# Second attention layer of a two-layer encoder: the heads as a written-out pipeline of 64 query-tile units

## The chip, the cores and the metric

One core of one Trainium2 chip runs the whole kernel. The metric is the device time of one execution in microseconds (us): 682.92 us is the median of three runs before the change (682.80 to 683.17). Five engines work side by side, each through its own list of instructions: TensorE (PE in the profile; PEld is its weight load), VectorE (DVE), ScalarE (ACT), GpSimd (POOL) and the queue that issues transfers (SP).

## The reference

Two encoder layers over 512 tokens of width 1024, in float32. The change lies in the second one, multi-head latent attention with 16 heads:

```python
def mixer_mla(xn, w_in, q_norm, w_qb, kv_norm, w_kvb, w_out):
    c_q, c_kv, k_rope, z = jnp.split(xn @ w_in, [384, 640, 672], axis=-1)
    q = (rmsnorm(c_q, q_norm) @ w_qb).reshape(B, S, H, 64 + 32)
    q_nope, q_pe = jnp.split(q, [64], axis=-1)
    q_pe = apply_rope(q_pe, cos, sin)
    kv = (rmsnorm(c_kv, kv_norm) @ w_kvb).reshape(B, S, H, 64 + 64)
    k_nope, v = jnp.split(kv, [64], axis=-1)
    k_pe = apply_rope(k_rope[:, :, None, :], cos, sin)
    ...
    o = block_attention(q, k, v)          # softmax(q k^T * 96 ** -0.5) v
    return (o.reshape(B, S, H * 64) * jax.nn.silu(z)) @ w_out
```

Around it stand the first layer (neighbourhood attention), the output projections, and after each layer a gated embedding: `h + sigmoid(rmsnorm(h) @ w_gate) * (p @ w_proj)`.

## The kernel before

**Precision.** Every float32 operand is split into two parts, `hi` and `lo` (`split`, L83 to L87: ScalarE copies to `hi`, VectorE or GpSimd subtracts to `lo`), and each product is three matmuls: hi by hi, hi by lo, lo by hi. A weight tile comes through `load_w` (L75 to L77): a transfer to `wraw`, the `hi` cast on ScalarE (L76, `whi`), the subtraction on GpSimd (L77, `wlo`). The pool `wp` has three buffers each of `wraw`, `whi` and `wlo`, so a fourth weight's cast can begin only when the matmuls that read one of the three are done.

**PSUM.** Eight banks of 128x512: two under the name `ps_mm` (projections), two `ps_S` (scores), three `ps_T` (transposes), one `ps_O` (a head's output).

**The second layer's heads (`mla_heads`, `mla_head`).** Heads go in eight pairs, and pairs in four groups of two.

- `group(g)` loads the group's weights (`mla_qr` for the rotary query part, `mla_kv` for keys and values, `mla_qn` for the queries), makes the rotary part (nine matmuls of 512 columns into one `ps_mm` bank; a copy, a lane shuffle, two products and a sum on ScalarE, VectorE and GpSimd; split to `rh`, `rl`), and the values of four heads (four times six matmuls of 256 columns, each evacuated by itself to a tile `vt`).
- `project(j)` makes one pair's operands: nine query matmuls into a `ps_mm` bank, evacuated by four instructions to `qe` and `qo` (the pair's even and odd head, hi and lo), six key matmuls into another, to `ke` and `ko`, and small transfers of rows of `rh` and `rl` into `qe` and `qo`.
- `attend(j)` runs the pair's two heads. A head has four query tiles. A tile's work: three score matmuls into `ps_S`; row maximum on VectorE (L594); exponential with row sum on ScalarE (L596); reciprocal (L597); scaling on GpSimd (L598); four transposes into `ps_T` (L122); split to `pt_hi` and `pt_lo`. After the four tiles come eight output matmuls into `ps_O`, four by `pt_hi` and four by `pt_lo`. `combine` (L182 to L185) evacuates the output, `gated` (L190 to L194) multiplies it by the gate `z` and splits it to `o1h`, `o1l`.

The gates of eight pairs (`z_phase`, 24 matmuls each) are made before the heads, the eighth between the first projection and the pairs. Behind the heads `ple` multiplies the layer's embedding (48 matmuls), then `out_proj` projects the output.

**What sets the order.** The program text calls for group, attention and projection one after the other; a scheduler with a timeline of its own then decides where each instruction stands on its engine, and may mix the scores of one head with the transposes of another. At run time each engine goes through its list in that order; an instruction waits on semaphores for its operands and for the buffer that it writes.

## Time and profile before

| | |
|---|---|
| median of 3 runs (range) | 682.92 us (682.80 to 683.17) |
| the profiled execution's own time | 682.41 us |
| span of the profile (first to last instruction) | 680.6 us |
| granted TensorE clock, mean over the span | 0.998 |
| stretch of the heads: first rotary matmul to the end of their mixing with `out_proj` | 404.8 to 590.0 us |

The profile's page gives the busy time of each engine, a chain of waits followed back from the last instruction, and groups of instructions by line. Answers on a stretch of time or a tile come from the same trace. A row of a timeline begins with start and length in us, then engine, line, operation, tile written <- tiles read, partitions x elements and the count merged. Matmuls overlap: the time that one costs in a row of them is the distance of two starts, not its length.

### The profile page before, as it was taken

The numbers are of one execution on the slowest core, as the hardware profiler recorded it, in microseconds if no ns is written. First come the engines' busy times: TensorE is split into PE (matmuls) and PEld (weight loads), VectorE is DVE, ScalarE is ACT, GpSimd is POOL, SyncE is SP. The second block draws the span as 40 slices with busy tenths as digits, with TensorE's granted clock in tenths as the row PEclk, the third lists the DMA queues.
The fourth block names the chain that finished last, engine by engine and source line by source line (L and its number), as shares of the span: only waits on it lengthen the run. The fifth ranks groups of instructions, "written<-read, shape, count | busy, mean of one in ns | idle before, by whom it ended". The sixth has DMA issues, their size and how long they took to land.

```text
span 680.6 us, 10112 instructions
## 1 busy us (share of the span) xinstructions
PE 660.7 (97%) x3552; PEld 564.2 (83%) x3552; DVE 369.4 (54%) x833; ACT 406.7 (60%) x808; POOL 395.2 (58%) x308
## 2 busy tenths in 40 slices
PE   6999999999999999999999999999999999999995
PEld 5888898988988888788999886787888777887885
DVE  6361555648646615724615404778888885046333
ACT  6753766657667643633444543888798877426423
POOL 0394556565766575832045634867799766658511
PEclk9999999999999999999999999999999999999999
DMA  8944214223142146434242252202121202584122
GB/s 276 375 139 145 89 41 136 87 93 111 40 137 74 63 176 231 166 110 149 93 128 93 75 160 80 82 23 93 26 70 39 86 1 78 203 296 154 60 78 93
DMA packets 30370, 79.10 MB, mean 116 GB/s; under 512 B 3952, under 2 KB 7280, under 8 KB 30320
## 3 DMA queue, kind: packets, MB, share of 16 engines
q1 hardware_dynamic: 30320, 78.47, 34.6%
q8 instruction: 28, 0.46, 0.3%
q14 instruction: 22, 0.18, 0.1%
HBM read 66.92 MB, written 8.39 MB: 111 GB/s over the span
## 4 chain that ended last, share of the span: by engine, by line
PE 87%; ACT 5%; DVE 3%; issue 2%; DMA 1%; POOL 1%; SPq 0%; POOLq 0%; DVEq 0%; ACTq 0%
PE ps_mm L96 60%; PE ps_S L96 10%; PE ps_T L122 5%; PE ps_O L96 4%; PE ps_O L357 2%; PE ps_mm L167 2%; PE ps_T L345 1%; ACT ex L596 1%; ACT whi L76 1%; PE ps_S L310 1%; PE ps_S L309 1%; DVE mx L594 1%; PE ps_T L96 1%; DMA wraw<-pT 1%; DMA wraw<-mla_c 0%
## 5 line engine op out<-in xcount | busy, mean ns | idle before, releaser
L77 POOL TENSOR_TENSOR wlo<-wraw,whi 128x1024 fp32r<-128x1024 f32 (+3 forms) x93 | 211.0, 2283 | 102.6 <-ACT whi L76 69.4
L76 ACT ACTIVATE whi<-wraw 128x1024 fp32r<-128x1024 f32 (+3 forms) x93 | 92.0, 999 | 80.1 <-PE ps_mm L96 20.1
L598 POOL TENSOR_TENSOR ex<-ex,rc 128x512 f32<-128x512 f32 x64 | 66.2, 1047 | 21.0 <-DVE rc L597 15.9
L96 PE MATMUL ps_mm<-whi,hnT 128*128 128x512 f32 (+1 forms) x272 | 69.7, 377 | 0.0
L96 PEld LDWEIGHTS ps_mm<-whi,hnT 128*128 128x128 f32 x272 | 49.5, 188 | 9.5
L332 POOL TENSOR_TENSOR ex<-ex,rc 128x128 f32<-128x128 f32 (+1 forms) x64 | 34.3, 560 | 37.9 <-DVE rc L328 36.4
L594 DVE TENSOR_REDUCE mx<-ps_S 128x1 f32<-128x512 f32 x64 | 43.7, 685 | 15.3 <-PE ps_S L96 14.4
L596 ACT ACTIVATE ex<-ps_S,mx 128x512 f32<-128x512 f32 x64 | 44.1, 689 | 8.2 <-DVE mx L594 6.7
L85 DVE TENSOR_TENSOR pt_lo<-ps_T,pt_hi 128x512 fp32r<-128x512 f32 x64 | 43.0, 679 | 5.0 <-ACT pt_hi L83 4.6
L327 ACT ACTIVATE ex<-ex,mx 128x128 f32<-128x128 f32 (+1 forms) x64 | 30.2, 473 | 21.5 <-DVE mx L323 21.2
L83 ACT ACTIVATE pt_hi<-ps_T 128x512 fp32r<-128x512 f32 x64 | 37.0, 598 | 7.6 <-PE ps_T L122 7.3
L96 PE MATMUL ps_mm<-xh,whi 128*128 128x512 f32 x152 | 41.0, 400 | 0.1
L96 PE MATMUL ps_mm<-wlo,hnT 128*128 128x512 f32 (+1 forms) x136 | 40.6, 379 | 0.0
L96 PE MATMUL ps_mm<-xh,wlo 128*128 128x512 f32 x152 | 39.2, 392 | 0.0
L96 PE MATMUL ps_mm<-xl,whi 128*128 128x512 f32 x152 | 38.7, 392 | 0.0
L122 PE MATMUL ps_T<-ident,ex 128*128 128x128 f32 x256 | 36.3, 273 | 0.2 <-DVE pt_lo L85 0.2
L122 PEld LDWEIGHTS ps_T<-ident,ex 128*128 128x128 f32 x256 | 30.7, 140 | 6.7 <-issue 0.7
L437 DVE TENSOR_TENSOR sg<-pe,sg 128x512 f32<-128x512 f32 (+1 forms) x17 | 12.5, 733 | 39.6 <-ACT sg L436 39.6
L96 PEld LDWEIGHTS ps_mm<-xl,whi 128*128 128x128 f32 x152 | 28.1, 188 | 5.7
L96 PEld LDWEIGHTS ps_mm<-xh,wlo 128*128 128x128 f32 x152 | 28.1, 188 | 5.5
L190 POOL TENSOR_TENSOR u<-u,z 128x512 f32<-128x512 f32 x16 | 20.6, 1290 | 19.6 <-DVE u L185 18.8
L106 POOL TENSOR_TENSOR rs<-ss,half 128x1 f32<-128x1 f32 x20 | 10.8, 549 | 35.9 <-DVE ss L105 34.7
(268 smaller groups left out, 1666.6 us busy)
## 6 DMA issues: line engine op xcount, KB each, us to landing
pe<-pe SPq DMA_DIRECT2D x32, 256.0 KB, 3.1
wraw<-na_qk SPq DMA_DIRECT2D x16, 512.0 KB, 3.3
wraw<-gate SPq DMA_DIRECT2D x16, 512.0 KB, 3.3
wraw<-na_v SPq DMA_DIRECT2D x8, 512.0 KB, 3.3
wraw<-na_o SPq DMA_DIRECT2D x8, 512.0 KB, 3.5
wraw<-mla_z SPq DMA_DIRECT2D x8, 512.0 KB, 3.6
wraw<-mla_o SPq DMA_DIRECT2D x8, 512.0 KB, 3.9
wraw<-na_z SPq DMA_DIRECT2D x6, 512.0 KB, 6.3
```

Source lines behind the costliest of these rows:

```text
L76: nc.scalar.activation(hi[:, c], raw[:, c], AF.Copy)
L77: (rest or nc.gpsimd).tensor_tensor(out=lo[:, c], in0=raw[:, c], in1=hi[:, c].bitcast(F32), op=ALU.subtract)
L83: nc.scalar.activation(hi, src, AF.Copy, scale=scale)
L85: nc.vector.tensor_tensor(out=lo, in0=src, in1=hi.bitcast(F32), op=ALU.subtract)
L96: last = nc.tensor.matmul(out, l, r, start=i == 0, stop=i == n - 1)
L122: self.nc.tensor.transpose(t[:, i * P:(i + 1) * P], b, self.ident)
L190: nc.gpsimd.tensor_tensor(out=u, in0=u, in1=z, op=ALU.mult)
L327: self.last_exp = nc.scalar.activation(e, e, AF.Exp, bias=mx[:, qt:qt + 1], accum_out=sm[:, qt:qt + 1])
L332: nc.gpsimd.tensor_tensor(out=e, in0=e, in1=rc[:, qt:qt + 1].to_broadcast([P, e.shape[1]]), op=ALU.mult)
L594: nc.vector.reduce_max(mx[:, c], sp, axis=AX.X, negate=True)
L596: nc.scalar.activation(ex, sp, AF.Exp, bias=mx[:, c], accum_out=sm[:, c])
L598: nc.gpsimd.tensor_tensor(out=ex, in0=ex, in1=rc[:, c].to_broadcast([P, S]), op=ALU.mult)
```

## The change

`mla_heads` is written anew. `group`, `project`, `attend` and `mla_head` are gone. A loop over 69 steps takes their place; its first 64 each handle one query tile (a unit) of one head. In step `i` TensorE gets, in this order: the scores of unit `i`, some matmuls of the next pair's operands (`pieces`), the transposes of unit `i-3`, and at two of four steps half of an earlier head's output (the half by `pt_hi` or the half by `pt_lo`). Each of these blocks is put behind the last matmul before it (`issue_after`), which fixes the order on TensorE alone; the other engines' order remains the scheduler's.

Further: the weights of a group are loaded in two halves (`parts=2`); two token tiles of values share a bank and are evacuated together; the rotary product with the cosine reads the bank instead of the copy; the products of `ple` are cut into 16 half blocks and put into the last steps, with the two output halves of a token tile stored together; for the first pair the values take `ps_S` banks, and the eighth gate stands wholly before the first scores.

```diff
+        def part(key, bank, terms, a0, a1):
+            if a0 == 0:
+                PS[key] = self.psum(bank)
+            for i in range(a0, a1):
+                self.last_mm = nc.tensor.matmul(PS[key], *terms[i], start=i == 0, stop=i == len(terms) - 1)
+            return PS.pop(key) if a1 == len(terms) else None
...
+        def load(key, ap, n):
+            W_[key] = self.load_w(ap, n, parts=2)
...
+        def rope(g, a0, a1):
+            psr = part(("r", g), "mm", q_terms(W_["qr", g], 0), a0, a1)
+            if psr is None:
+                return
...
             nc.scalar.activation(xr, psr, AF.Copy)
             nc.vector.stream_shuffle(sw, xr, swap)
-            nc.vector.tensor_tensor(out=xr, in0=xr, in1=rc_t, op=ALU.mult)
+            nc.vector.tensor_tensor(out=xr, in0=psr, in1=rc_t, op=ALU.mult)
...
+        def queries(j, a0, a1, bank="mm"):
+            g, jj = j // 2, j % 2
+            psq = part(("q", j), bank, q_terms(W_["qn", g], jj * 384), a0, a1)
+            if psq is None:
+                return
             st = sets[j % 2]
+            for dst, r in ((st["qe"], slice(0, 64)), (st["qo"], slice(64, 128))):
                 self.split(dst[0][r], dst[1][r], psq[r], QSC)
...
+        def pieces(j):
+            n, g = j + 1, j // 2 + 1
+            w = [[] for i in range(8)]
+            add = lambda i, f, *x: w[i].append(lambda: f(*x))
+            if j < 6 and j % 2 == 0:
+                add(0, queries, n, 0, 2)
+                add(1, queries, n, 2, 8)
+                add(2, queries, n, 8, 9)
+                add(2, load_kv, g)
+                add(2, keys, n, 0, 5)
+                add(3, keys, n, 5, 6)
+                add(3, load_qn, g)
+                add(3, rope, g, 0, 1)
+                add(4, rope, g, 1, 3)
+                add(5, rope, g, 3, 9)
+                add(6, values, g, 0)
+                add(6, values, g, 1)
+            elif j < 7:
+                add(0, queries, n, 0, 1)
+                add(1, queries, n, 1, 6)
+                add(2, queries, n, 6, 9)
+                if j == 6:
+                    add(2, load, "w0", a["proj"][1, 0], 1024)
+                add(2, keys, n, 0, 2)
+                add(3, keys, n, 2, 3)
+                add(4, keys, n, 3, 4)
+                add(5, keys, n, 4, 6)
+                if j == 6:
+                    add(5, load, "w1", a["proj"][1, 1], 1024)
+                    add(6, ple)
+                    add(6, ple)
...
+        for i in range(69):
+            work = []
+            if i < 64:
+                work.append(lambda: score(i))
+                work += pieces(i // 8)[i % 8]
+            elif i < 66:
+                work += [ple, ple]
+            if 3 <= i < 67:
+                work.append(lambda: turn(i - 3))
+            if i >= 7 and i % 4 in (3, 0):
+                work.append(lambda: output((i - 7) // 4, (i + 1) % 4))
+            for f in work:
+                with self.tc.issue_after(self.last_mm.ins):
+                    f()
```

`score`, `turn` and `output` hold what `mla_head` held, for one unit, one unit and half a head. Rows that precede the second layer's heads are the same on every engine.

Two places in the lists matter below. The first is TensorE in the third pair (units 16 to 23), where the next group's rotary product begins; `ps_mm_4836` are the keys of the fourth pair (its queries, `ps_mm_4770`, end just ahead), `ps_mm_4872` is the rotary product, and `ps_S` are scores. Before, the corresponding place (rotary product `ps_mm_4992`) reads:

```order
L96 MATMUL ps_O_4669<-pt_lo_4604,vt_4247 128x512
L96 MATMUL ps_O_4669<-pt_lo_4604,vt_4257 128x512
L96 MATMUL ps_S_4814<-ke00_3497,qe00_3493 128x512
L96 MATMUL ps_S_4814<-ke01_3498,qe00_3493 128x512
L96 MATMUL ps_S_4814<-ke00_3497,qe01_3494 128x512
L96 MATMUL ps_mm_4992<-cT0_3491,whi_4987 128x512 x3
L96 MATMUL ps_mm_4992<-cT1_3492,whi_4987 128x512 x3
L96 MATMUL ps_mm_4992<-cT0_3491,wlo_4988 128x512 x3
L96 MATMUL ps_S_4830<-ke00_3497,qe00_3493 128x512
```

and now:

```order
L510 MATMUL ps_mm_4770<-cT0_3491,wlo_4415 128x512
L510 MATMUL ps_mm_4836<-cT0_3491,whi_4385 128x512 x2
L510 MATMUL ps_mm_4836<-cT1_3492,whi_4385 128x512 x2
L510 MATMUL ps_mm_4836<-cT0_3491,wlo_4386 128x512
L122 MATMUL ps_T_4842<-ident_70,ex_4740 128x128 x4
L96 MATMUL ps_S_4849<-ke00_3497,qe00_3493 128x512
L96 MATMUL ps_S_4849<-ke01_3498,qe00_3493 128x512
L96 MATMUL ps_S_4849<-ke00_3497,qe01_3494 128x512
L510 MATMUL ps_mm_4836<-cT0_3491,wlo_4386 128x512
L510 MATMUL ps_mm_4872<-cT0_3491,whi_4720 128x512
L122 MATMUL ps_T_4876<-ident_70,ex_4766 128x128 x4
```

Nine rotary matmuls in one piece have become one, two and six in three steps, and the first of them follows the last query matmul after only six key matmuls, four transposes and three score matmuls.

The second place is ScalarE over the same steps. `whi_4828` and `whi_4864` are casts of the next group's key and value weights and query weights, `ex` the exponentials, `pt_hi` the split of transposes, `qe10`, `qo10`, `ke10`, `ko10` the evacuation of the fourth pair's queries and keys. Before (casts `whi_5014`, `whi_5060`):

```order
L596 ACTIVATE ex_4704,sm_4679<-ps_S_4699,mx_4678 128x512
L76 ACTIVATE whi_5014<-wraw_5013 128x1024
L83 ACTIVATE qe10_3501<-ps_mm_4957 64x512
L76 ACTIVATE whi_5060<-wraw_5059 128x768
L83 ACTIVATE ke10_3505<-ps_mm_4975 64x512
L596 ACTIVATE ex_4720,sm_4679<-ps_S_4715,mx_4678 128x512
L83 ACTIVATE pt_hi_4603<-ps_T_4662 128x4x128
L83 ACTIVATE pt_hi_4681<-ps_T_4692 128x4x128
L83 ACTIVATE qo10_3503<-ps_mm_4957 64x512
```

and now:

```order
L599 ACTIVATE ex_4766,sm_4759<-ps_S_4761,mx_4758 128x512
L83 ACTIVATE pt_hi_4744<-ps_T_4773 128x4x128
L187 ACTIVATE u_4784<-ps_O_4753 64x512
L76 ACTIVATE whi_4828<-wraw_4827 128x512 x2
L599 ACTIVATE ex_4792,sm_4759<-ps_S_4787,mx_4758 128x512
L83 ACTIVATE pt_hi_4744<-ps_T_4802 128x4x128
L83 ACTIVATE qe10_3501<-ps_mm_4770 64x512
L599 ACTIVATE ex_4814,sm_4759<-ps_S_4809,mx_4758 128x512
L76 ACTIVATE whi_4864<-wraw_4863 128x384 x2
L83 ACTIVATE pt_hi_4744<-ps_T_4842 128x4x128
L83 ACTIVATE qo10_3503<-ps_mm_4770 64x512
L83 ACTIVATE ke10_3505<-ps_mm_4836 64x512
```

Both lists have the two casts ahead of evacuations; now each cast is in two halves, and the first stands ahead of the exponential of unit 17 (`ex_4792`), whose scores TensorE finishes before the last query matmuls.

## The prediction

> **What bounds the kernel now.** I read the page first, then the windows of the heads' stretch, then TensorE's timeline, then the chain of waits where that timeline has holes.

> ```profile
> PE 660.7 (97%) x3552; PEld 564.2 (83%) x3552; DVE 369.4 (54%) x833; ACT 406.7 (60%) x808; POOL 395.2 (58%) x308
> PE 87%; ACT 5%; DVE 3%; issue 2%; DMA 1%; POOL 1%; SPq 0%; POOLq 0%; DVEq 0%; ACTq 0%
> ```

> The span is 680.6 us. TensorE has 97% of it and 87% of the chain: only its own work or its waits can move the end. The lists before and after hold the same 3552 matmuls, so its work stays; what can change is how long it waits. Busy time hides that, since matmuls overlap, so I count. The stretch (its length, then busy time and instructions of PE, PEld, DVE, ACT, POOL, then the granted clock), and its matmuls that are not 512 columns wide:

> ```profile
> 404.80:590.00 185.20, 179.16 (x940) 147.03 (x939) 131.82 (x268) 140.77 (x300) 134.39 (x108) 1.00 0.22 67
> ```

> ```profile
> L122 PE MATMUL ps_T<-ident,ex 128*128 128x128 f32 x256 | 36.3, 273 | 0.2 <-DVE pt_lo L85 0.2
> ...
> L96 PE MATMUL ps_mm<-whi,cT 128*128 128x256 f32 x64 | 10.8, 291 | 1.2 <-DVE vt L85 0.8 <-ACT xr L518 0.3
> ...
> L96 PE MATMUL ps_mm<-wlo,cT 128*128 128x256 f32 x32 | 6.4, 282 | 0.0
> ```

> That leaves 940 - 256 - 96 = 588 matmuls of 512 columns. What one costs in a row of them is the distance of starts, from TensorE's timeline where it does not wait:

> ```profile
> 505.37 0.86 PE L96 MATMUL ps_S<-ke,qe 96*128 96x512 f32 x3
> 506.07 0.60 PE L122 MATMUL ps_T<-ident,ex 128*128 128x128 f32 x4
> 506.43 0.94 PE L96 MATMUL ps_S<-ke,qe 96*128 96x512 f32 x3
> ...
> 514.07 0.64 PE L96 MATMUL ps_mm<-whi,cT 128*128 128x256 f32 x4
> 514.55 0.40 PE L96 MATMUL ps_mm<-wlo,cT 128*128 128x256 f32 x2
> 514.79 0.60 PE L122 MATMUL ps_T<-ident,ex 128*128 128x128 f32 x4
> ```

> ```profile
> 365.02 10.94 PE ps_mm L96 x48
> ```

> The second fence is a row of the chain: 48 matmuls of 512 columns in 10.94 us, 0.228 each. Three scores take 0.70 (505.37 to 506.07), four transposes 0.36, six matmuls of 256 columns 0.72, half an output 4 x 0.23 = 0.92. Work of the stretch: 588 x 0.228 = 134.1, 96 x 0.12 = 11.5, 64 x 0.36 = 23.0, together 168.6 us of 185.2. **TensorE waits about 16 us there**; that is all the change can win, and 682.9 - 16 = 667 is the floor. A hole shows how these waits come about, in the chain:

> ```profile
> 456.98 0.66 ACT ex L596 x2
> 457.64 0.95 ACT whi L76
> 458.59 0.46 ACT qe L83
> 459.05 0.74 ACT whi L76
> ...
> 460.15 0.79 ACT ex L596 x2
> ...
> 460.98 0.97 PE ps_S L96 x3
> ```

> Two weight casts (0.95 and 0.74) and an evacuation stand in ScalarE's list between two exponentials; the scores at 460.98 start right behind the second, which frees their bank. ScalarE runs its list in order, so whatever waits at its head holds all behind it. Over the stretch such casts waited for TensorE, too:

> ```profile
> L76 ACT ACTIVATE whi<-wraw 128x1024 fp32r<-128x1024 f32 (+2 forms) x17 | 15.7, 925 | 6.2 <-PE ps_mm L96 6.1
> ```

> **The change, by its steps.** A step's matmuls, first four steps of a pair that prepares a group: 0.70 + 2 x 0.23 + 0.36 + 0.92 = 2.44; 0.70 + 6 x 0.23 + 0.36 = 2.44; 0.70 + 6 x 0.23 + 0.36 = 2.44; 0.70 + 2 x 0.23 + 0.36 + 0.92 = 2.44. Each unit thus has three steps, some 7.3 us, from scores to transposes. The chain between is maximum, exponential, reciprocal and scaling:

> ```profile
> L594 DVE TENSOR_REDUCE mx<-ps_S 128x1 f32<-128x512 f32 x64 | 43.7, 685 | 15.3 <-PE ps_S L96 14.4
> L598 POOL TENSOR_TENSOR ex<-ex,rc 128x512 f32<-128x512 f32 x64 | 66.2, 1047 | 21.0 <-DVE rc L597 15.9
> L87 DVE SCALAR_TENSOR_TENSOR qo<-ps_mm,qo 64x512 fp32r<-64x512 f32 x8 | 5.6, 695 | 0.9 <-ACT qo L83 0.7
> L521 POOL TENSOR_TENSOR sw<-sw,rope_s 128x512 f32<-128x512 f32 x4 | 6.1, 1520 | 0.0
> L522 POOL TENSOR_TENSOR xr<-xr,sw 128x512 f32<-128x512 f32 x4 | 5.2, 1290 | 0.9 <-DVE xr L520 0.7
> L77 POOL TENSOR_TENSOR wlo<-wraw,whi 128x1024 fp32r<-128x1024 f32 (+3 forms) x93 | 211.0, 2283 | 102.6 <-ACT whi L76 69.4
> ```

> 0.69 + 0.9 + 0.2 + 1.05 is under 3 us, so transposes rarely wait. What binds instead are banks and ScalarE's list. Its distances of starts:

> ```profile
> 456.85 0.70 ACT L596 ACTIVATE ex<-ps_S,mx 128x512 f32<-128x512 f32 x1
> ...
> 457.51 1.08 ACT L76 ACTIVATE whi<-wraw 128x1024 fp32r<-128x1024 f32 x1
> 458.46 0.59 ACT L83 ACTIVATE qe<-ps_mm 64x512 fp32r<-64x512 f32 x1
> 458.94 0.85 ACT L76 ACTIVATE whi<-wraw 128x768 fp32r<-128x768 f32 x1
> 459.67 0.59 ACT L83 ACTIVATE ke<-ps_mm 64x512 fp32r<-64x512 f32 x1
> ```

> An exponential takes 0.66, a key-and-value cast 0.95 (1.0 in two halves, my estimate), a query cast 0.73 (0.75 in halves), an evacuation 0.48.

> *The rotary product's bank.* In pairs 2 and 4, counted from the pair's first score, the last query matmul ends at 4.88 + 0.70 + 0.23 = 5.81, and the first rotary matmul is due at 8.25. It takes the query bank, so it needs the pair's `qo` evacuated. On ScalarE the key-and-value cast has stood at the head since about 3.3: its buffer comes free with the last query matmul. From 6.0 on (0.2 for the result to land) come in order: cast 1.0, exponential 0.66, `pt_hi` 0.48, `qe` 0.48, exponential 0.66, query cast 0.75, `pt_hi` 0.48, `qo` 0.6 to its result, which makes 11.1, and VectorE's `qo` 0.70: 11.8. TensorE stands from 8.25 to 11.8: **3.5 us, twice**; all scores, transposes and outputs queue behind. If ScalarE's backlog were half, 1.2; with GpSimd late as well, 4.5. In pair 0, without transposes, the same sum gives 8.6 against 6.25: **2.4**, and 0.3 for a score bank.

> *Pair 6* (counting from 0) loads `proj` behind its queries and keys. The cast of 1.0 delays `pt_hi`, and the output half at its fourth step waits **1.3**; the second cast waits for the last key matmul ahead of an exponential, and the seventh step's scores wait **2.1**.

> *Output halves.* At the end of a pair, the first half comes 0.70 + 0.36 after the transposes that it needs, while `pt_hi` follows others on ScalarE: 0 to 0.8 each, seven times, **3**.

> *The eighth gate* now follows the first keys and takes the query bank. Its weights' buffer comes free with the rotary matmuls; from there cast 0.95, GpSimd 2.28, rotary product 1.52 and sum 1.29, which `rh`, then `ke` and `qo` follow on ScalarE (1.6), then 0.70: 10.9 after the last early gate, against 8.3 for the keys' end: **2.6** (1.5 to 3.5).

> *At nothing:* values in pairs (half the evacuations), the cosine product from the bank, loads in halves (some 14 casts more, 0.05 each) and joined stores lie beside TensorE, on engines that are busy 132 to 141 us of 185. If ScalarE were full, the halves would cost 0.7. On SP the loads' transfers need only a `wraw` buffer, which the subtraction frees several steps sooner than the casts' buffers come free, so they land ahead of the casts; behind SP's small transfers of `rh` and `rl` stand only loads for later steps.

> *The end.* `proj`'s buffers are held to the last half blocks, so `out_proj`'s first cast starts only then: 0.95 + 2.28 for the lower part, under 3.4 us of blocks and transposes and 2.7 of its first twelve matmuls. Small waits there and in pair 7: **0.8**.

> Sum: 3.5 x 2 + 2.7 + 3.4 + 3 + 2.6 + 0.8 = 19.5 us of waits in place of 16: +3.5. Against the profiled 682.41 this is 685.9; the runs' median lies 0.5 above the profiled one, so **686.5 us**. With every term at its low end the waits are some 11, at its high end 27: 678 to 694.

> [...]

> **The rivals.** *Faster: the fixed order finds its operands ready.* The place is the rotary product's first matmul and the point is `qo`: if ScalarE's list flows there and `qo` is evacuated 2.4 us after the queries' end, the 9.4 us of rotary waits go. 10 us remain, 6 under the 16 now: 677. For it: three steps between scores and transposes, engines 71 to 76% busy. Against it: the order of ScalarE's list, and 6.1 us of casts already waiting for TensorE in the old one.

> *No change:* both sets of waits come out at 16, within 1.4 us, 682.9. For it speaks that the same casts and evacuations share the same ScalarE; against it that nothing ties the two sums.

> *Slower still: the clock.* When TensorE stands, its granted clock falls, at least at the end:

> ```profile
> 670.00:681.00 11.00, 3.33 (x28) 0.86 0.26 95
> ```

> Of these 11.00 us TensorE is busy 3.33, and the clock's mean is 0.86.

> The holes of this stretch, at most 1.6 us, left it at 1.00. Holes of 3.5 are longer. If each of the two lowered it to half, matmuls at twice 0.228 for one step add some 2.4 us each: 691.

> [...]

> **How the numbers follow.** Forecast 0.46; faster 0.34; no change 0.13; clock 0.07. About 0.2%, 1.4 us, is what a measurement of this kernel tells from no change: 681.5 to 684.3. So faster 0.34, same 0.13, slower 0.53. The forecast's own range is 684.3 to 691. The faster case spreads from 667 to 681.5, mostly above 674; I leave out a little below that, and above 692. Range 674 to 692.

> **What would show it.** For the forecast: the first rotary matmul of a group idle by 2 to 4 us, released by VectorE's `qo`; ScalarE idle before the casts, released by TensorE; waits of TensorE in the stretch of 17 to 24 us. For the faster rival: no hole over 1 us behind the eighth gate, and evacuations within 2.4 us. For the clock: granted clock under 1.00 in a window between 430 and 580. The forecast is wrong if `qo` lands before the rotary matmul is due, or if TensorE's waits fall under 14 us.

## The result, and the profile after

| | before | after |
|---|---|---|
| median of 4 runs each, on one chip (range) | 682.86 us (682.56 to 683.17) | 688.52 us (687.91 to 691.05) |
| ratio to before, 95% interval | | 1.0090 (1.0064 to 1.0116) |
| the profiled execution's own time, and its span | 682.41, 680.6 us | 691.05, 689.3 us |
| mean granted clock over the span | 0.998 | 0.992 |

The kernel became 0.9% slower, 5.7 us. The profiled execution of the changed kernel is the longest of its four; the other three have a mean clock of 0.994 and take 687.91 to 688.91 us. One more stretch at half clock, which by the estimate of 1.7 us below would lower the mean clock by 0.002, fits the 0.992 and covers more than half of that difference; the other three left no trace.

The page's busy time and chain after the change:

```profile
PE 663.9 (96%) x3552; PEld 567.6 (82%) x3552; DVE 370.3 (54%) x825; ACT 408.5 (59%) x815; POOL 395.6 (57%) x323
PE 86%; ACT 7%; DVE 3%; issue 1%; DMA 1%; POOL 1%; SPq 0%; POOLq 0%; DVEq 0%; ACTq 0%
```

The shares hardly differ from before. The stretch of the heads tells more. Counted from the first rotary matmul over the same number of matmuls, 940, as the 185.20 us before (length, then busy time and instructions of each engine, then the clock):

```profile
406.67:598.60 191.93, 180.67 (x940) 149.21 (x939) 132.73 (x260) 141.04 (x302) 133.89 (x120) 0.98 0.22 72
```

It is 6.7 us longer, at a clock of 0.98. Where TensorE stands idle is told by its groups in 400 to 600 us: first the groups before the change that stand over 0.5 us (count, busy time, mean of one; then the idle time just before them and who ended it),

```profile
L96 PE MATMUL ps_S<-ke,qe 96*128 96x512 f32 x96 | 28.8, 409 | 2.1 <-ACT ex L596 1.4 <-ACT ke L83 0.7
L96 PE MATMUL ps_S<-ko,qo 128*128 128x512 f32 x96 | 28.8, 410 | 1.5 <-ACT ex L596 1.5
L96 PE MATMUL ps_O<-pt_hi,vt 128*128 128x512 f32 x64 | 18.0, 403 | 0.7 <-ACT pt_hi L83 0.7
```

(the values' 1.2 us stand in the prediction), and after it:

```profile
L510 PE MATMUL ps_mm<-cT,whi 128*128 128x512 f32 x104 | 31.3, 399 | 6.0 <-DVE qo L87 6.0
L616 PE MATMUL ps_O<-pt_hi,vt 128*128 128x512 f32 x64 | 19.2, 422 | 2.9 <-ACT pt_hi L83 2.8
L96 PE MATMUL ps_mm<-x1h,whi 128*128 128x512 f32 x16 | 4.9, 460 | 2.2 <-DVE qo L87 2.2
```

No scores wait for an exponential any more: the written-out order does what it says. In their place stand the rotary product (6.0 us in three waits, all for VectorE's `qo`), the first output halves (2.9 us, for `pt_hi`) and the eighth gate (2.2 us, for `qo` of the first queries): 11.1 us in place of 5.5.

The wait of the third pair (pair 2) in the timeline, all three engines; rows go by engine, and `[2.16 <-DVE qo L87]` is idle time ahead of an instruction and who ended it:

```profile
466.58 0.40 PE L510 MATMUL ps_mm<-cT,wlo 128*128 128x512 f32 x1
...
468.31 0.95 PE L96 MATMUL ps_S<-ke,qe 96*128 96x512 f32 x3
469.10 0.40 PE L510 MATMUL ps_mm<-cT,wlo 128*128 128x512 f32 x1
471.65 0.47 PE L510 MATMUL ps_mm<-cT,whi 128*128 128x512 f32 x1 [2.16 <-DVE qo L87]
...
465.17 1.15 ACT L76 ACTIVATE whi<-wraw 128x512 fp32r<-128x512 f32 x2 [0.84 <-PE ps_mm L510]
466.35 0.69 ACT L599 ACTIVATE ex<-ps_S,mx 128x512 f32<-128x512 f32 x1
...
467.02 0.59 ACT L83 ACTIVATE pt_hi<-ps_T 128x512 fp32r<-128x512 f32 x1
467.50 0.58 ACT L83 ACTIVATE qe<-ps_mm 64x512 fp32r<-64x512 f32 x1
467.98 0.68 ACT L599 ACTIVATE ex<-ps_S,mx 128x512 f32<-128x512 f32 x1
...
468.64 0.94 ACT L76 ACTIVATE whi<-wraw 128x384 fp32r<-128x384 f32 x2
469.47 0.59 ACT L83 ACTIVATE pt_hi<-ps_T 128x512 fp32r<-128x512 f32 x1
470.08 0.59 ACT L83 ACTIVATE qo<-ps_mm 64x512 fp32r<-64x512 f32 x1
...
468.25 0.67 DVE L87 SCALAR_TENSOR_TENSOR qe<-ps_mm,qe 64x512 fp32r<-64x512 f32 x1
...
470.81 0.69 DVE L87 SCALAR_TENSOR_TENSOR qo<-ps_mm,qo 64x512 fp32r<-64x512 f32 x1
```

The last query matmul starts at 466.58; VectorE's `qo` ends at 471.50, 4.92 us later, and the rotary product, which writes that bank, starts at 471.65. From 465.17 on ScalarE has no idle time until `qo`, and these rows start in the order of its list under the change.

The clock is the second part. Six stretches of 3.41 us, TensorE alone (length, busy time and instructions, granted clock):

```profile
414.88:418.29 3.41, 1.20 (x6) 1.00 0.27 65
418.29:421.71 3.42, 3.42 (x10) 0.50 0.30 71
469.50:472.91 3.41, 1.26 (x8) 1.00 0.44 154
472.91:476.32 3.41, 3.41 (x11) 0.50 0.37 115
510.44:513.85 3.41, 1.86 (x11) 1.00 0.07 15
513.85:517.27 3.42, 2.80 (x14) 1.00 0.36 138
```

Behind the gate's wait (2.21 us, to 417.38) and behind the wait of pair 2 (2.16 us, to 471.65) TensorE runs 3.41 us at a clock of 0.50: three scores take 1.28 us to the next start there (473.66 to 474.94), against 0.68 at a clock of 1.00 (477.41 to 478.09). Reckoned by the clock, it does in 3.41 us what 1.71 us would do. Behind the wait of pair 4 (third pair of rows) the clock stays at 1.00, though a wait of the same length stands there (2.17 us, to 514.47). So in this execution the clock takes, by this estimate, 2 x 1.7 = 3.4 us. Beside the work as the prediction prices it, 168.6 us, there remain 191.93 - 168.6 - 3.4 = 19.9 us, against 185.20 - 168.6 = 16.6 before.

The prediction calls this remainder waits, but not all of it is. By the busy times in the two rows of the stretch TensorE is idle for 191.93 - 180.67 = 11.3 us, and before the change for 185.20 - 179.16 = 6.0. The other 8.6 and 10.6 us are in large part work priced too low: the three scores at 468.31 in the timeline above, which wait for nothing, take 0.79 us to the next start and not 0.70. Averaged over all matmuls of 512 columns that follow one another without idle time, a step is 0.24 us in the traces of both kernels where 0.228 was taken, which makes 6 to 7 us.

### The profile page after: what moved, and what is told of

It reads as the page before. It is cut to its first block, busy times and chain, and to the rows that moved or that the text cites. A ratio compares the mean times of both kernels' runs of the same rounds, so it can differ in the third digit from the quotient of the medians.

```text
span 689.3 us, 10135 instructions
## 1 busy us (share of the span) xinstructions
PE 663.9 (96%) x3552; PEld 567.6 (82%) x3552; DVE 370.3 (54%) x825; ACT 408.5 (59%) x815; POOL 395.6 (57%) x323
## 4 chain that ended last, share of the span: by engine, by line
PE 86%; ACT 7%; DVE 3%; issue 1%; DMA 1%; POOL 1%; SPq 0%; POOLq 0%; DVEq 0%; ACTq 0%
PE ps_mm L96 54%; PE ps_S L96 10%; PE ps_mm L510 5%; PE ps_T L122 5%; PE ps_O L616 5%; PE ps_O L360 2%; ACT ex L599 2%; PE ps_mm L167 2%; PE ps_T L348 1%; PE ps_S L313 1%; PE ps_S L312 1%; ACT whi L76 1%; ACT pt_hi L83 1%; PE ps_T L96 1%; DMA wraw<-pT 1%
## 5 line engine op out<-in xcount | busy, mean ns | idle before, releaser
L77 POOL TENSOR_TENSOR wlo<-wraw,whi 128x1024 fp32r<-128x1024 f32 (+5 forms) x108 | 213.0, 1989 | 107.3 <-ACT whi L76 75.7
L76 ACT ACTIVATE whi<-wraw 128x1024 fp32r<-128x1024 f32 (+5 forms) x108 | 93.2, 886 | 74.8 <-PE ps_mm L96 19.8
L601 POOL TENSOR_TENSOR ex<-ex,rc 128x512 f32<-128x512 f32 x64 | 66.2, 1042 | 29.0 <-DVE rc L600 10.6
L96 PE MATMUL ps_mm<-whi,hnT 128*128 128x512 f32 (+1 forms) x272 | 69.7, 377 | 0.0
L96 PEld LDWEIGHTS ps_mm<-whi,hnT 128*128 128x128 f32 x272 | 49.5, 188 | 9.5
L335 POOL TENSOR_TENSOR ex<-ex,rc 128x128 f32<-128x128 f32 (+1 forms) x64 | 34.4, 562 | 37.9 <-DVE rc L331 36.3
L597 DVE TENSOR_REDUCE mx<-ps_S 128x1 f32<-128x512 f32 x64 | 44.0, 688 | 21.2 <-PE ps_S L96 19.7
L599 ACT ACTIVATE ex<-ps_S,mx 128x512 f32<-128x512 f32 x64 | 43.7, 683 | 13.4 <-DVE mx L597 13.2
L85 DVE TENSOR_TENSOR pt_lo<-ps_T,pt_hi 128x512 fp32r<-128x512 f32 x64 | 43.1, 685 | 11.7 <-ACT pt_hi L83 10.9
L83 ACT ACTIVATE pt_hi<-ps_T 128x512 fp32r<-128x512 f32 x64 | 37.4, 596 | 8.0 <-PE ps_T L122 7.8
L96 PE MATMUL ps_mm<-xh,whi 128*128 128x512 f32 x152 | 41.0, 400 | 0.1
L96 PE MATMUL ps_mm<-wlo,hnT 128*128 128x512 f32 (+1 forms) x136 | 40.6, 379 | 0.0
L96 PE MATMUL ps_mm<-xh,wlo 128*128 128x512 f32 x152 | 39.2, 392 | 0.0
L96 PE MATMUL ps_mm<-xl,whi 128*128 128x512 f32 x152 | 38.7, 392 | 0.0
L122 PE MATMUL ps_T<-ident,ex 128*128 128x128 f32 x256 | 38.5, 274 | 0.1
L122 PEld LDWEIGHTS ps_T<-ident,ex 128*128 128x128 f32 x256 | 31.8, 142 | 7.5 <-POOL ex L601 0.5
L510 PE MATMUL ps_mm<-cT,whi 128*128 128x512 f32 x104 | 31.3, 399 | 6.0 <-DVE qo L87 6.0
L188 DVE TENSOR_TENSOR u<-ps_O,u 64x512 f32<-64x512 f32 x32 | 22.0, 686 | 24.6 <-ACT u L187 24.1
L96 PEld LDWEIGHTS ps_mm<-xl,whi 128*128 128x128 f32 x152 | 28.1, 188 | 5.7
L96 PEld LDWEIGHTS ps_mm<-xh,wlo 128*128 128x128 f32 x152 | 28.1, 188 | 5.5
```

The costliest lines, as they stand in the source:

```text
L76: nc.scalar.activation(hi[:, c], raw[:, c], AF.Copy)
L77: (rest or nc.gpsimd).tensor_tensor(out=lo[:, c], in0=raw[:, c], in1=hi[:, c].bitcast(F32), op=ALU.subtract)
L83: nc.scalar.activation(hi, src, AF.Copy, scale=scale)
L85: nc.vector.tensor_tensor(out=lo, in0=src, in1=hi.bitcast(F32), op=ALU.subtract)
L96: last = self.last_mm = nc.tensor.matmul(out, l, r, start=i == 0, stop=i == n - 1)
L122: self.last_mm = self.nc.tensor.transpose(t[:, i * P:(i + 1) * P], b, self.ident)
```

## The experiments

Ten kernels, in three rounds on one chip each with the kernel before beside them. Its medians there are 683.24, 683.50 and 682.94 us, against 682.86 in the first comparison, which alone holds the kernel after; so a difference of times from two sets can be off by some 0.6 us. The idle columns are the groups of TensorE's rows in 400 to 600 us, as above: rotary product for `qo`, first output half for `pt_hi`, eighth gate for `qo`, scores for an exponential.

| | median (range), us | ratio to before (95%) | rotary | output | gate | scores |
|---|---|---|---|---|---|---|
| after | 688.52 (687.91 to 691.05) | 1.0090 (1.0064 to 1.0116) | 6.0 | 2.9 | 2.2 | 0.0 |
| 1 rotary product later | 683.62 (681.22 to 684.40) | 1.0002 (0.9987 to 1.0016) | 0.6 | 3.3 | 2.2 | |
| 2 casts behind | 688.63 (686.16 to 690.86) | 1.0071 (1.0047 to 1.0096) | 5.3 | 3.5 | 2.2 | |
| 3 gate's bank | 685.90 (685.05 to 688.01) | 1.0038 (1.0024 to 1.0052) | 6.0 | 2.9 | 0.0 | 0.0 |
| 4 waits filled | 686.33 (684.66 to 687.48) | 1.0041 (1.0028 to 1.0053) | 1.9 | 2.9 | 0.1 | 0.0 |
| 5 `qo` first | 685.38 (683.28 to 686.64) | 1.0024 (1.0011 to 1.0038) | 2.1 | 3.0 | 2.2 | |
| 6 = 1 + 3 | 678.83 (678.66 to 680.21) | 0.9936 (0.9922 to 0.9950) | 0.6 | 3.3 | 0.0 | 0.0 |
| 7 = 6, output half later | 675.99 (675.46 to 676.58) | 0.9890 (0.9876 to 0.9904) | 0.6 | 0.0 | 0.0 | 0.8 |
| 8 two and two | 685.12 (683.66 to 685.82) | 1.0029 (1.0020 to 1.0039) | 2.4 | 4.2 | 1.4 | |
| 9 = 8, casts behind | 686.15 (685.59 to 686.86) | 1.0047 (1.0032 to 1.0062) | 1.3 | 5.9 | 1.4 | |
| 10 = 7, two and two | 682.18 (680.96 to 682.50) | 0.9985 (0.9976 to 0.9995) | 0.0 | 3.6 | 0.0 | 2.9 |

(Empty: under 0.3 us. In run 4 the idle time is what is left beside the extra matmuls.)

### Round one: each suspect alone

**1. The rotary product one step later.**

```diff
-                add(3, rope, g, 0, 1)
-                add(4, rope, g, 1, 3)
+                add(4, rope, g, 0, 3)
```

> The rotary product starts one step later (its first matmul moves from a pair's fourth step to the fifth), nothing else moves on TensorE. Theory A (the query bank is not free yet because the evacuation of qo stands behind casts on ScalarE): the waits ahead of the first rotary matmul in pairs 0, 2 and 4 (1.9, 2.3 and 2.3 us) fall under 0.4 us each, and the half-clock window behind pair 2's wait goes with its hole: 688.5 - 6 - 1.7 = about 681, at most 683. Rival B (ScalarE is short of time in these steps, so the wait only changes its place): scores or output halves wait instead, and the time stays within 1.5 us of 688.5.

683.62, so 4.9 us less. The rotary waits fell to one short one, in pair 0:

```profile
L510 PE MATMUL ps_mm<-cT,whi 128*128 128x512 f32 x104 | 30.2, 393 | 0.6 <-DVE qo L87 0.6
```

Hardly any of it returned (output halves from 2.9 to 3.3), so the wait was a real loss: rival B falls, and the loss hung on the place of one matmul. The median missed 681 to 683 by a little. The rotary waits fell by 5.4 us, as expected; the clock's share was taken too high, since the profile of this kernel still has the half-clock stretch behind the gate (0.50 from 416.77 to 420.19 us), and the median after the change holds little more than one such stretch (2.2 us by run 4, at 1.7 each). Of its ten executions the one with a mean clock of 0.998 took 681.22 us.

**2. The casts behind the `qo` evacuation**, TensorE's list unchanged.

```diff
+            self.qo_cast = self.cast
...
+            with self.tc.issue_after(self.qo_cast.ins) if g else nullcontext():
                 load(("kv", g), a["mla_kv"][g], 1024)
...
+            with self.tc.issue_after(self.qo_cast.ins) if g else nullcontext():
                 load(("qn", g), a["mla_qn"][g], 768)
```

> The casts of the next group's two weights stand behind the qo evacuation in ScalarE's list; TensorE's list is unchanged row for row. Theory A: qo is evacuated some 2.4 us after the queries' end, the first rotary matmul waits under 0.5 us in pairs 0, 2 and 4, and the time is 681 to 683.5. Rival B (qo is late anyway, behind exponentials and pt_hi): the rotary waits stay over 1.5 us each and the time is 687 or more. Rival C (the casts then come too late for the values in the seventh step): the rotary waits go, but the first value matmul waits over 1 us in each of the three pairs: 684 to 688.

688.63: theory A, the prediction's own, falls. The times spread with the clock: the two executions with a mean clock of 0.998 took 686.16 and 686.42 us, the five at 0.991 to 0.994 took 687.24 to 690.86. The timeline at the same place:

```profile
466.24 0.40 PE L510 MATMUL ps_mm<-cT,wlo 128*128 128x512 f32 x1
...
471.12 0.47 PE L510 MATMUL ps_mm<-cT,whi 128*128 128x512 f32 x1 [1.96 <-DVE qo L87]
...
466.67 0.59 ACT L83 ACTIVATE qe<-ps_mm 64x512 fp32r<-64x512 f32 x1 [0.34 <-PE ps_mm L510]
...
468.25 0.60 ACT L83 ACTIVATE pt_hi<-ps_T 128x512 fp32r<-128x512 f32 x1 [0.25 <-PE ps_T L122]
468.88 0.59 ACT L83 ACTIVATE qo<-ps_mm 64x512 fp32r<-64x512 f32 x1
...
468.96 0.69 DVE L600 TENSOR_REDUCE mx<-ps_S 128x1 f32<-128x512 f32 x1 [0.57 <-PE ps_S L96]
469.56 0.68 DVE L85 TENSOR_TENSOR pt_lo<-ps_T,pt_hi 128x512 fp32r<-128x512 f32 x1
470.28 0.69 DVE L87 SCALAR_TENSOR_TENSOR qo<-ps_mm,qo 64x512 fp32r<-64x512 f32 x1
```

No cast stands there, ScalarE even has idle time, and still VectorE's `qo` ends 4.73 us after the last query matmul's start, 0.2 sooner than with the casts. On ScalarE `qo` stands behind the `pt_hi` of transposes that come after the queries; on VectorE behind the maximum of scores that come after them, and behind `pt_lo`. Both lists take the bank's four readers and the units' own work by turns.

**3. The eighth gate in a bank of the transposes**, which have no work yet.

```diff
-        zs.update(self.z_phase(a["mla_z"], xT, range(NEARLY, 8)))
+        zs.update(self.z_phase(a["mla_z"], xT, range(NEARLY, 8), bank="T"))
```

> The eighth gate takes a bank of the transposes, which have no work yet, in place of the first queries' bank. Theory A (the gate waits for the bank, that is for the evacuation of the first queries): the wait of 2.4 us ahead of the gate goes, and the half-clock window behind it (1.7 us) goes too: 684 to 686. Rival B (the gate's weights are late): the wait stays, 688.5.

685.90, as theory A has it: the wait was for the bank, not for the gate's weights.

**4. The waits filled**, with matmuls whose result is not used.

```diff
+        def fill():
+            t = self.psum("T")
+            for i in range(6):
+                self.last_mm = nc.tensor.matmul(t, ch[:, 0, 0:P], ch[:, 0, :], start=i == 0, stop=i == 5)
...
+                add(3, fill)
                 add(3, rope, g, 0, 1)
```

> Six extra matmuls of 512 columns into a spare bank (1.4 us, their result is not used) stand ahead of the eighth gate and ahead of the first rotary matmul of pairs 0, 2 and 4, inside the waits. Theory C (a wait of over 2 us in one window of 3.4 us puts the next window at half clock, 1.7 us each): the waits' ends stay where they were, the idle parts shrink to about 1 us, no window between 400 and 590 us has a granted clock under 1.00, and the time falls by about 3.4 us to 685 (684.5 to 686.5). Rival D (half-clock windows have another cause, or cost nothing since the engine would wait anyway): windows of half clock remain or the time stays within 1 us of 688.5. Rival E (the extra matmuls delay TensorE): 690 or more.

686.33, 2.2 us less, with 24 matmuls more. The two windows behind whose waits the clock had fallen (length, TensorE's busy time and instructions, clock):

```profile
410.00:420.00 10.00, 9.88 (x50) 1.00 0.46 132
...
470.00:480.00 10.00, 9.84 (x57) 1.00 0.28 93
```

After the change the same two windows had TensorE busy 7.79 and 8.35 us at clocks of 0.91 and 0.83. Theory C holds here: with the waits filled the clock stays at 1.00 in both, and as they are not shortened the rest of the loss is left. The 3.4 us expected are those of the profiled execution; against the median it is 2.2. 686.3 is also what the change costs by its waits alone: 3.1 us over the 683.24 of the kernel before in these runs.

### Round two: what delays `qo`, and the gains together

**5. `qo` ahead of the next unit's work on both engines**, on top of run 2.

```diff
+                    if i < 48 and i // 8 % 2 == 0 and (i % 8 == 3 or i % 8 == 2 and done):
+                        order.enter_context(self.tc.issue_after(self.qo_cast.ins))
+                        order.enter_context(self.tc.issue_after(self.qo_rest.ins))
```

> As the run with the casts behind the evacuation, and besides qo's two instructions stand ahead of the next unit's work: on ScalarE ahead of pt_hi, on VectorE ahead of the maximum and pt_lo. TensorE's list is unchanged. Theory F (not the casts alone delay qo, but the unit's own pt_hi, maximum and pt_lo that stand ahead of it in the two lists): qo lands about 2.4 us after the queries' end, the first rotary matmul waits under 0.5 us in pairs 0, 2 and 4, and the time is 681 to 683.5. Rival G (those instructions, now later, delay TensorE just as much): waits of 1 to 2 us appear at scores, transposes or output halves of these steps, and the time stays at 686 or more.

685.38, between the two theories. The rotary waits fell to 2.1 us in sum, and `qo` ends 3.4 us after the last query matmul's start in place of 4.7:

```profile
463.37 0.40 PE L510 MATMUL ps_mm<-cT,wlo 128*128 128x512 f32 x1
...
464.78 0.67 DVE L87 SCALAR_TENSOR_TENSOR qe<-ps_mm,qe 64x512 fp32r<-64x512 f32 x1
...
465.48 0.59 ACT L83 ACTIVATE qo<-ps_mm 64x512 fp32r<-64x512 f32 x1 [0.35 <-DVE qe L87]
...
466.11 0.69 DVE L87 SCALAR_TENSOR_TENSOR qo<-ps_mm,qo 64x512 fp32r<-64x512 f32 x1 [0.59 <-ACT qo L83]
```

Here ScalarE's `qo` waits for nothing but VectorE's `qe`, 0.35 us. In the program ScalarE's `qo` carries a semaphore wait for VectorE, in both the old and the new kernel (0.27 us at 487.45 before the change), though it reads other rows of the bank and writes another tile: both programs keep the four readers of this bank one behind the other. Four of them by turns pass between the two lists three times.

**6. Runs 1 and 3 together.**

> The rotary product one step later and the eighth gate in a bank of the transposes, both together. If the two waits are separate losses, their gains add: 688.5 - 4.9 - 2.6 = 681.0 (680 to 682), faster than the kernel before by some 2 us, with no half-clock window between 400 and 590 us. Rival: they share a part (the clock), and it is 682 to 684.

678.83, below the expected 680 to 682: the gains add, and more. The edits are worth 4.9 and 2.6 us alone, 9.7 together. Each alone leaves one wait that the profiled execution shows followed by half clock (run 1 behind the gate, 0.50 from 416.77 to 420.19 us; run 3 behind pair 2's wait, 0.50 from 466.59 to 470.00); with both edits the profiled execution's mean clock is 0.998, as before the change, against 0.996 and 0.994, and it is 0.996 to 0.998 in all five. That fits the surplus of 2.2 us, though only one execution of each was profiled.

**7. Also the first output half at a pair's end, behind the next pair's scores.**

```diff
             if i < 64:
                 work.append(lambda: score(i))
+                if i % 8 == 0 and i:
+                    work.append(lambda: output((i - 8) // 4, 0))
...
-            if i >= 7 and i % 4 in (3, 0):
+            if i >= 7 and i % 4 in (3, 0) and (i % 8 != 7 or i > 56):
```

> As the run before, and the first output half at a pair's end comes behind the next pair's first scores. Theory H (the half waits for the last pt_hi of its head, since only three scores and four transposes cover it there): the waits of 1.0 us (pairs 1, 3, 5) and 0.4 to 0.5 us (pairs 2, 4, 6) go: 4.5 us less than the run before, 676 to 678. Rival I (the next pair's scores then come 0.9 us sooner and wait for their bank instead): within 1.2 us of the run before.

675.99 us: 1.1% faster than the kernel before. How the half waited in the changed kernel, and the groups of this run:

```profile
457.97 0.60 ACT L83 ACTIVATE vt<-ps_mm 128x512 fp32r<-128x512 f32 x1
458.47 0.68 ACT L599 ACTIVATE ex<-ps_S,mx 128x512 f32<-128x512 f32 x1
...
459.12 1.08 ACT L83 ACTIVATE pt_hi<-ps_T 128x512 fp32r<-128x512 f32 x2
...
459.77 0.96 PE L616 MATMUL ps_O<-pt_hi,vt 128*128 128x512 f32 x3 [0.77 <-ACT pt_hi L83]
```

```profile
L96 PE MATMUL ps_S<-ke,qe 96*128 96x512 f32 x96 | 29.4, 414 | 0.8 <-ACT ex L599 0.8
...
L616 PE MATMUL ps_O<-pt_hi,vt 128*128 128x512 f32 x64 | 18.0, 403 | 0.0
```

The 3.3 us of the output halves went; 0.8 of it came back at scores that wait for an exponential (rival I, in small), so 2.8 was gained where theory H had 4.5. The same 940 matmuls now take

```profile
405.11:583.20 178.09, 176.61 (x940) 147.17 (x939) 132.13 (x260) 140.89 (x302) 134.11 (x121) 1.00 0.25 78
```

178.1 us, and TensorE is idle in only 178.09 - 176.61 = 1.5 of them.

### Round three: the order within an evacuation

**8. Both of ScalarE's instructions first, then both of VectorE's**, in the kernel after the change.

```diff
-            for dst, r in ((st["qe"], slice(0, 64)), (st["qo"], slice(64, 128))):
-                self.split(dst[0][r], dst[1][r], psq[r], QSC)
+            both = (st["qe"], slice(0, 64)), (st["qo"], slice(64, 128))
+            for dst, r in both:
+                self.cast = nc.scalar.activation(dst[0][r], psq[r], AF.Copy, scale=QSC)
+            for dst, r in both:
+                nc.vector.scalar_tensor_tensor(dst[1][r], psq[r], QSC, dst[0][r].bitcast(F32), op0=ALU.mult, op1=ALU.subtract)
```

> One edit in the kernel after the change: the queries' evacuation is written as both ScalarE instructions and then both VectorE ones (qe, qo; qe, qo) in place of qe, qe, qo, qo by turns. The program then has no wait of ScalarE's qo for VectorE's qe, and the query bank passes between the two engines' lists once in place of three times. TensorE's list and the casts' places are unchanged. Theory J (qo is late because the bank's four readers follow each other across two lists, each time behind a unit's own work): ScalarE's qo follows qe at once, VectorE's qo lands some 1.5 us sooner, the rotary waits fall from 2.3 to under 1 us, the eighth gate's wait falls by about 1 us, and the time is 682 to 684.5. Rival (the casts at the head of the list are the delay): the waits stay over 1.8 us, 687 or more.

The mechanism is shown, with the casts where they were:

```profile
462.38 0.40 PE L510 MATMUL ps_mm<-cT,wlo 128*128 128x512 f32 x1
...
466.07 0.47 PE L510 MATMUL ps_mm<-cT,whi 128*128 128x512 f32 x1 [0.77 <-DVE qo L574]
...
463.31 0.58 ACT L572 ACTIVATE qe<-ps_mm 64x512 fp32r<-64x512 f32 x1
463.91 0.59 ACT L572 ACTIVATE qo<-ps_mm 64x512 fp32r<-64x512 f32 x1
...
465.23 0.69 DVE L574 SCALAR_TENSOR_TENSOR qo<-ps_mm,qo 64x512 fp32r<-64x512 f32 x1
```

`qo` ends 3.54 us after the last query matmul's start in place of 4.92, and the gate waits 0.8 us less. The time missed the range, 685.12: the output halves wait 1.3 us more in sum, since the two evacuations now stand in one piece ahead of `pt_hi`.

Whether ScalarE's `qo` could do without waiting for VectorE's `qe` was not shown: no run here leaves that wait out; run 8 only orders around it.

**9. The same with the casts behind.**

> The same edit, and the casts behind the qo evacuation. Theory J: the casts now matter, since they are what is left ahead of the pair of instructions: 1.15 us sooner again, rotary waits under 0.3 us, 681 to 682.5. If the run with the evacuation alone already has no waits over 0.5 us, the two are equal within 1 us.

686.15 where 681 to 682.5 was expected: no gain. The rotary waits fell to 1.3 us, and the output halves took 5.9. The casts take their 2 us of ScalarE somewhere in these steps; behind `qo` they stand ahead of the `pt_hi` that the output half needs.

**10. Run 7 with queries and keys two and two.**

> The run with the rotary product later, the gate's bank and the output half later (676.0), with both queries' and keys' evacuations two and two. No wait over 0.8 us is left there for a bank, so it should stay within 0.7 us of 676; if scores wait for evacuations in the many small holes, 1 to 2 us less.

682.18, 6.2 us slower than run 7: the largest miss of this round. Only 0.6 us waited for `qo` there any more, so the edit had little to win, and the pieces of two instructions hold up `pt_hi` (3.6 us of waits in place of none) and the exponentials (2.9 in place of 0.8).

## Why the prediction held, and where it did not

**The sum of waits** came out near the forecast in part by luck. Reckoned as in the prediction it is 19.9 us where 19.5 was forecast, 3.3 more than before where 3.5 was. But two errors offset each other. The terms of the sum are holes, and the holes measure 11.3 us, not 19.5: the rotary product was priced 3.7 too high, pair 6 by 3.4 and the end by 0.8 for nothing, the gate 0.4 too high. And the 16 us that the sum was set against were not holes alone, but 6.0 us of idle time and 10.6 of other costs, in large part work priced too low. The holes grew by 5.3 us and the other costs shrank by 2.0; what shrank them is not shown. So the direction and three of the places were foreseen, and the agreement of 3.3 with 3.5 was chance.

**The time** is 2.0 us above the 686.5, and that is the clock: with the waits filled (run 4, clock 1.00 in every window of 10 us from 400 to 590 us) the kernel takes 686.3.

**The rotary product** waits in pairs 0, 2 and 4, for VectorE's `qo`, as named. The size was too large: the rows show 6.0 us where the terms were 2.7 + 7.0. The step that was mis-sized is when the key-and-value cast may begin. It was taken to wait for the last query matmul; it began at 465.17, after 0.84 us of idle time ended by a matmul of `ps_mm`, ahead of the last query matmul at 466.58. The three matmuls by `wlo` that end the queries do not read the cast's buffer `whi`, so that came free with the last one that does. Behind it the list ran as written, without a gap.

**The cause** was half right. That ScalarE's list sets `qo` is shown; that the casts at its head do it is not. Run 2 took them away and 0.2 us changed; the bank's readers behind the units' own work are a second reason, nearly as long, which the sum contained (it listed the exponentials and `pt_hi` ahead of `qo`) but the words did not weigh. Runs 5 and 8 each shorten it by 1.3 to 1.4 us. The faster rival's condition, `qo` 2.4 us after the queries' end, was not reached: `qo` ended 3.43 us after the last query matmul's start in run 5, 3.54 in run 8, which is 3.0 and 3.1 us after that matmul's end.

**Pair 6** was priced at 3.4 us and shows no such wait: no scores wait at all, and the `pt_hi` waits are accounted for by the pair ends. Its casts, too, began sooner, in keeping with the reason just named: the first at 549.64 us, ahead of the three query matmuls by `wlo` at 550.27, the second at 555.28, behind the key matmul by `whi` at 554.85 and ahead of the last two by `wlo` at 557.14.

**The output halves** (3 forecast, 2.9 measured) and **the eighth gate** (2.6 forecast, 2.2 measured) were right in place and size. For the gate the reason holds: run 3 shows the bank, and in the trace GpSimd's rotary sum ends at 414.45 us, `rh` starts at 414.48, `ke` and `qo` follow on ScalarE, VectorE's `qo` ends at 417.23, and the gate starts at 417.38. (The terms listed for it, behind nine rotary matmuls, add up to 10.4 and not 10.9, so to a wait of 2.1.) **The end** (0.8 forecast) shows no wait, and **at nothing** stayed at nothing: beside the three groups shown, no group of TensorE's rows in 400 to 600 us has more than 0.1 us of idle time.

**The clock** was listed as a rival at 0.07, on the condition of holes of 3.5 us. It came on top of the forecast's waits, behind two of three holes of 2.2 us, at 1.7 us each and not 2.4: the clock of 0.50 lasted 3.41 us and cost, as reckoned above, half of it. So it belonged into the sum, as a term of about 2 us, not beside it.

**The change itself** gained what it aimed at, scores that no longer wait (3.6 us before), and gave it back at three places where TensorE's fixed order asks for a bank or an operand one step too early. Runs 6 and 7 move those three and keep the rest: 675.99.

## What to carry to other kernels

When an order is fixed by hand, every instruction that claims a bank needs a distance to the last reader of that bank (the rotary product of pair 2 waited 2.16 us for it), and that distance is not the evacuation's own time but its place in the lists of both evacuating engines: here 4.9 us for four instructions of about 0.6. Moving the one claiming instruction was worth more than reordering the engines it waits for, which in runs 8 and 9 handed part of the wait to the next reader. And waits should be added up together with the clock: behind two of the three holes of 2.2 us in TensorE's work the clock was 0.50 for 3.41 us, by the estimate above another 1.7 us each.

## What the runs showed of the hardware

The two half-clock stretches among the heads after the change are 3.41 us long. In the 3.41 us ahead of each TensorE was busy 1.20 and 1.26 us; in those ahead of 513.85, where the clock stayed at 1.00, 1.86 us. Two other runs give a pair of rows each. Run 2, behind pair 2's wait (length, TensorE's busy time, clock):

```profile
469.17:472.58 3.41, 1.46 (x9) 1.00 0.00 0
472.58:476.00 3.42, 3.42 (x12) 0.50 0.53 161
```

Run 5, around the gate's wait of 2.2 us; the mean clock of this execution is 0.998:

```profile
412.58:415.99 3.41, 1.48 (x7) 1.00 0.31 90
415.99:419.41 3.42, 3.14 (x14) 1.00 0.45 106
```
